# A two-model program on one core: TensorE's instructions in the order of the source, in place of the scheduler's order

## The chip, the cores and the metric

The program runs on one core of one Trainium2 chip. The metric is the device time of one execution in microseconds (us), the median of several runs. A core has five engines with instruction queues of their own: TensorE (PE: matrix products; its weight loads are listed apart as PEld), VectorE (DVE), ScalarE (ACT), GpSimd (POOL) and SyncE (SP, which here only starts transfers). Sixteen DMA engines bring the weights from memory.

## The reference

Two models run one after the other's parts on 256 tokens of width 1024. The first is one hybrid block (state-space scan, sparse attention, mixture of 32 experts), the second two layers that work on a sequence `x` and a context `ctx` (grouped-query attention, then latent attention, each with a convolutional feed-forward network). Cut to what matters here:

```
hn = rmsnorm(h) * (1 + scale1) + shift1               # ada = silu(c) @ w_ada gives shifts, scales, gates
y_ssm = mamba2(hn @ w_z, hn @ w_xbc, hn @ w_dt) @ w_ssm_out
y_nsa = nsa(hn @ w_q, keys, values, gates) @ w_nsa_out
h = h + gate1 * ((sigmoid(hn @ w_gs) * y_ssm + sigmoid(hn @ w_ga) * y_nsa) @ w_o)
hn2 = rmsnorm(h) * (1 + scale2) + shift2
for e in range(32):                                    # two experts of each token count
    out += combine[:, e] * ((silu(hn2 @ w_g[e]) * (hn2 @ w_u[e])) @ w_d[e])
h = h + gate2 * out
# second model, per layer: x, ctx += gate * mixer(norm(x), norm(ctx)); x, ctx += gate * ffn(...)
# layer 0: q, k = rms_norm per head, rope on x; softmax(q k^T) v over ctx and x keys; layer 1: MLA
out = final norms of both, joined
```

All inputs are fp32, and the products are held close to fp32.

## The kernel before

**Products.** A dense product is worked in groups of 512 KB to 1 MB of weights. `weight` starts a transfer from SP's queue into one of 14 buffers `raw` (256 KB each); ScalarE rounds it into `whi` (L212), VectorE puts the rest into `wlo` (L213), four buffers of each; `mm3` then issues three matmuls (L241, L242, L243: whi by the high part, wlo by the high part, whi by the low part). The three stand for one product below and are called a triple. `lin_fm` issues 8 triples for a group, 256 columns wide; `lin_tm` does the same with tokens on the partitions. `behind` holds the products of a group back in the source until the split of the next group has been issued, and evictions of a finished sum are put off in the same way (`late`, `flush`).

**Small matmuls in fours.** Experts get 32 rows of a 128-row tile each: `expert_block` issues for every slice of the contraction four fp32 matmuls of 32 columns, one for each expert of the unit, that write different quarters of one bank (L1346 for gate and up, L1368 for down). The modulation vectors (L417) do the same with four slices of 512 columns. These are called quads below. The trace counts an fp32 matmul as two instructions, so that a whole quad is x8 there and x4 in the order of the program.

**The order of the work.** The source is written as generators. `weave` advances one (the main one) and after each step lets the others (fills) run for the cost that the step announced, by shares written in the code (`CTX`, `COST`, `Gap`). So products that wait for nothing but their weights stand in the source between the steps of chains that wait for other engines. This is not the order that runs: the Tile framework's scheduler orders each engine's instructions anew when the program is built, by its own estimate of when an operand is ready and with the source's order as the priority. The order is fixed then; at run time every engine goes through its queue in order.

**The stages.** First `first_act` and `project_tm` (dense projections, up to 79 us), then `project_xbc`, the gates `ssg` and `sga` with the scan (`ssd`) and the sparse attention (`nsa`) woven in, the scan's norm (`ssd_norm`, L798 and L548), the output products, the router, the experts (to about 1077 us) with the context half of layer 0 woven in, the attention of layer 0 on `x` (heads: norm, rope, transposes L1632; scores L1744), its feed-forward part, layer 1 and the final norms. In the experts stage `experts_rest` is a conditional block (`tc.If`) that runs only if an expert was chosen more often than its places allow.

Of the kernel before, what the change touches and what calls it, by code (L numbers as in the profile page):

```python
# [107 lines left out]
class Kernel:  # L108
# [932 lines left out]
    def tanh_gates(self, act, c0, sg):  # L1041
# [2 lines left out]
            self.A.activation(sg[:, m, :], ps, AF.Tanh, scale=0.5)  # L1044
        yield from self.lin_fm(self.I["w_in"][0], c0, D, act, ev)

    def mark(self, name):
        self.marks.append(name)

    def first_block(self, rb):  # L1050
        V, A, T, I = self.V, self.A, self.T, self.I
        h = self.h
        act, pss = self.first_act(rb)
        self.mark("tm")
        self.drain(self.project_tm(act, pss))
        self.rope_tables()
        self.ssd_dt()
        self.mark("xbc")
        self.load_vecs([3, 4, 5, 6, 7])
        for i in range(2):  # L1060
            self.take_bias(self.fetch_bias(self.I["ada_b_2"][i]), self.ada2[i])
        prep = self.nsa_prepare()
        self.mix(self.project_xbc(act), (prep, 0.1))
        self.drain(prep)

        def nsa():
            yield from self.nsa_compress()
            self.nsa_cmp_probs()
            yield 2.0
            yield from self.nsa_attend()  # L1070
        ssg = self.sb("F", [P, 8, TOK], name="ssg")
        nsa_g, ssd_g, ada_g = nsa(), self.ssd(), self.ada_rest
        self.mark("ssg")
        self.mix(self.tanh_gates(act, 6992, ssg), (ssd_g, 0.7), (nsa_g, 0.35), (ada_g, 0.3))
        sga = self.sb("G", [P, 8, TOK], name="sga")
        self.mark("sga")
        self.mix(self.tanh_gates(act, 8016, sga), (ssd_g, 0.6), (nsa_g, 0.35), (ada_g, 0.3))
        self.drain(ssd_g)
        self.mark("z")
        sums = [self.sb(f"cbm{i}", [P, 2, TOK], name="sums") for i in range(2)]  # L1080
        self.mix(self.ssd_gate(act, sums), (nsa_g, 0.55), (ada_g, 0.3))
        self.drain(nsa_g)
        self.mark("norm")

        def ev_a(m, ps):
            V.scalar_tensor_tensor(sga[:, m, :], sga[:, m, :], 1.0, ps, OP.add, OP.mult)
        norm = self.ssd_norm(sums)
        self.mix(self.lin_fm(I["w_nsa_out"][0], 0, D, self.nsa, ev_a), (norm, NORM), (ada_g, 0.2))
        self.drain(norm)
        self.mark("out")  # L1090

        class Two:
            def __init__(self, ts):
                self.ts = ts

            def __getitem__(self, key):
                _, k, s = key
                return self.ts[k // 8][:, k % 8, s]

        mh, ml = self.pair("B", [P, 8, TOK])  # L1100

        def ev_s(m, ps):
            V.scalar_tensor_tensor(ssg[:, m, :], ssg[:, m, :], 1.0, ps, OP.add, OP.mult)
            V.tensor_tensor(sga[:, m, :], sga[:, m, :], ssg[:, m, :], OP.add)
            self.evict_split(mh[:, m, :], ml[:, m, :], sga[:, m, :])
        self.mix(self.lin_fm(I["w_ssm_out"][0], 0, D, (Two(self.y_hi), Two(self.y_lo)), ev_s), (ada_g, 0.3))
        self.drain(ada_g)
        ctx = self.layer0_ctx_in()
        next(ctx)
        g = self.sb("s", [P, 8])  # L1110
        V.tensor_scalar(g, self.ada1[:, 0, 16:24], 0.5, None, OP.mult)
        self.mix(self.residual(I["w_o"][0], (mh, ml), h, g), (ctx, CTXIN))
        self.drain(ctx)
        self.dbg("h1", h)
# [197 lines left out]
    def expert_weights(self, part, experts):  # L1312
# [20 lines left out]
        return tiles  # L1333

    def expert_block(self, xg, d, q, experts, sizes):

        V, A, T = self.V, self.A, self.T
        tiles = [slice(sum(sizes[:j]), sum(sizes[:j + 1])) for j in range(len(sizes))]
        acc = self.ps("acc", [P, 512])
        for i in range(4):  # L1340
            for n in "gu":
                ws = self.expert_weights(n + str(i), experts)
                c0 = 256 * (n == "u")
                for k in range(2):
                    for r, w in zip(tiles, ws):
                        T.matmul(acc[r, c0:c0 + 256], xg[:, 2 * i + k, P * q + r.start:P * q + r.stop], w[:, k, :],  # L1346
                                 start=(n == "g" and i == 0 and k == 0), stop=(i == 3 and k == 1), skip_group_check=True)
                yield COST[len(sizes)]
# [61 lines left out]
    def experts(self):  # L1410

        xs, first, n = {}, {}, 0
        for unit in sorted(UNITS.split()):
            first[unit] = n
            n += len(SIZES.get(unit, [32] * 4))
        for unit in UNITS.split():
            d, q = int(unit[0]), int(unit[1])
            if d not in xs:
                xs[d] = self.expert_gather(d, f"XB{len(xs) % 2}")
                yield 1.0  # L1420
            sizes = SIZES.get(unit, [32] * 4)
            ids = self.ids(self.order, range(first[unit], first[unit] + len(sizes)))
            yield from self.expert_block(xs[d], d, q, ids, sizes)
            if unit == REST:
                self.experts_rest()

    def experts_rest(self):

        self.settle()
        total = self.nc.values_load(self.over[0:1, 16:17], min_val=0, max_val=16)  # L1430
        with self.tc.If(total > 0):
            for d in (6, 7):
                xg = self.expert_gather(d, f"XB{d % 2}")
                for q in range(2):
                    n = 8 * (d - 6) + 4 * q
                    self.drain(self.expert_block(xg, d, q, self.ids(self.over, range(n, n + 4)), [32] * 4))
# [487 lines left out]
    def run(self):  # L1924
        with self.tc.tile_pool(name="sb", bufs=1) as self.pool:
            self.setup()
            self.h = self.sb("hx", [P, 8, TOK])
            self.ada1 = self.sb("ada1", [P, 1, 48])
            self.ada2 = [self.sb(f"ada2{i}", [P, 2, 48]) for i in range(2)]
            for tag in SHARED:  # L1930
                if tag == SHARED[tag]:
                    self.sb(tag, [P, 8, TOK])
            with self.phase(cw2=2, pb=5, pT=2), self.banks(lin=2, fl=1, S=2, aux=2, acc=1):
                first = [self.fetch_vecs(0)]
                x = self.fetch_tm(self.I["x"][0], "C", self.A)
                self.take_vecs([0], first)
                self.ada_stat()
                bias = self.fetch_bias(self.I["b_ada"][0])
                first = [self.fetch_vecs(1)]
                self.turn_fm(x, self.h)  # L1940
                self.load_constants(0)
                rb = self.sb("rb", [P, TOK])
                self.V.tensor_copy(rb, self.rms_bcast(self.h, 8, D))
                self.take_vecs([1], first)
                self.take_bias(bias, self.ada1)

                def rest():
                    yield from self.ada_first([1, 2])
                    yield from self.ada_second(0)
                self.ada_rest = rest()  # L1950
                self.first_block(rb)
            with self.phase(k4=4, m=3, fg=2, hT=2):
                with self.banks(lin=2, S=2, aux=2, acc=2):
                    self.load_constants(1)
                    self.mark("router")
                    ctx = self.layer0_ctx()
                    self.mix(self.router(self.h), (ctx, CTX[0]))
                    self.mark("experts")
                    self.mix(self.experts(), (ctx, lambda: CTX[1 + self.room // 2]))
                    self.mark("L0")  # L1960
                    self.mix(self.layer0_x_attend(), (ctx, lambda: CTX[3 + (self.att is not None)]))
                    self.mark("ctx rest")
                    self.drain(ctx)
                with self.banks(lin=4, fl=1, aux=2, acc=1):
                    self.mark("L0 rest")

                    def side():
                        yield from self.ada_second(1, Q2)
                        yield from self.layer1_ctx()
                    ctx = side()  # L1970
                    self.mix(self.layer0_x_rest(), (ctx, 0.5))
                    self.drain(ctx)
                    self.ada_last = self.ada_second(1, Q3)
                    self.mark("L1")
                    self.drain(self.layer1_x())
                    self.finish()


# [29 lines left out]
```

## Time and profile before

| what | value |
|---|---|
| median of three runs | 1915.17 us (1913.99, 1915.17, 1926.64) |
| the profiled execution, its own time | 1915.28 us |
| its span | 1913.5 us, so 1.8 us lie around it |
| PE, PEld, DVE, ACT busy | 95%, 74%, 67%, 48% |
| DMA | 381.53 MB, mean 199 GB/s |
| mean granted TensorE clock | 0.975 of full speed |

The busy time of an engine is the time in which at least one of its instructions runs, by a model of the ends for PE. The clock is a share of 2.4 GHz, the higher of two levels. Rows of a timeline give the start, the duration, the engine, the line and the operation, output before inputs; neighbours of one kind are merged, with their count behind x.

### The profile page before, as it was taken

The page shows a single profiled execution, that of the slowest core. Times are in us where ns is not written, and L with a number is a line of the kernel's source. Part 1 is how long each engine was busy: PE and PEld are TensorE (multiplying, and loading weights), DVE is VectorE, ACT ScalarE, POOL GpSimd, SP SyncE. Part 2 cuts the span into 40 slices and gives each one's busy share as a digit, 9 for nine tenths or more (in the row PEclk, how much of TensorE's full clock was granted, in tenths as well). Part 3 has the DMA queues.
Part 4 walks back from the last instruction along what each step waited for, and adds up shares of the span by engine and source line. Part 5 has one row for each costly group of instructions (what it writes and reads, how often), then busy time and mean ns, then how long its engine had stood idle before and what let it go on. Part 6 is the DMA issues. An engine that isn't in the chain of part 4 may idle for free.

```text
span 1913.5 us, 36458 instructions
## 1 busy us (share of the span) xinstructions
PE 1810.3 (95%) x12928; PEld 1411.7 (74%) x12928; DVE 1274.4 (67%) x3074; ACT 916.2 (48%) x1893; POOL 41.5 (2%) x48
## 2 busy tenths in 40 slices
PE   7999999999979989989989998998999989989998
PEld 3897767678855578756555675767999966479998
DVE  3997787765786367444433678837877877468776
ACT  3666457733544234212212356635655655347654
POOL 0000000100010000000000010000000000000000
PEclk9999999999999989999989998998999999999999
DMA  9757866579527949949787451274566553476662
GB/s 309 206 144 250 267 191 213 186 233 319 165 94 238 324 138 340 347 152 335 254 257 243 138 147 53 75 245 133 171 182 183 154 166 125 146 220 185 183 183 82
DMA packets 344961, 381.53 MB, mean 199 GB/s; under 512 B 27353, under 2 KB 298454, under 8 KB 344774
## 3 DMA queue, kind: packets, MB, share of 16 engines
q1 hardware_dynamic: 339456, 376.47, 63.2%
q10 hardware_dynamic: 5174, 1.97, 0.4%
q8 instruction: 104, 1.70, 0.4%
q14 instruction: 83, 0.68, 0.1%
q0 software_dynamic: 144, 0.71, 0.1%
HBM read 378.00 MB, written 1.05 MB: 198 GB/s over the span
## 4 chain that ended last, share of the span: by engine, by line
PE 47%; DVE 3%; DMA 2%; ACT 2%; issue 1%; POOL 1%; SPq 0%; POOLq 0%; DVEq 0%; ACTq 0%
PE lin L242 11%; PE lin L241 11%; PE lin L243 10%; PE acc L1346 3%; PE fl L417 2%; PE acc L1559 2%; PE acc L1368 2%; PE lin L1878 1%; PE aux L1551 1%; PE S L1744 1%; DMA raw<-in_ada_w_dram 1%; PE aux L1401 1%; DVE wlo L213 0%; POOL s L1612 0%; PE aux L1824 0%
## 5 line engine op out<-in xcount | busy, mean ns | idle before, releaser
L212 ACT CAST whi<-raw 128x512 fp32r<-128x512 f32 (+2 forms) x752 | 452.3, 610 | 446.3 <-PE lin L243 290.3
L213 DVE TENSOR_TENSOR wlo<-raw,whi 128x512 fp32r<-128x512 f32 (+2 forms) x752 | 501.8, 677 | 182.7 <-ACT whi L212 171.5
L241 PE MATMUL lin<-XA,whi 128*128 128x256 f32 x832 | 238.5, 287 | 2.2 <-ACT XA L494 2.2
L242 PE MATMUL lin<-XA,wlo 128*128 128x256 f32 x832 | 237.3, 285 | 0.0
L243 PE MATMUL lin<-XA,whi 128*128 128x256 f32 x832 | 237.0, 285 | 0.0
L241 PE MATMUL lin<-A,whi 128*128 128x256 f32 x576 | 168.3, 292 | 3.4 <-DVE k L627 3.4
L241 PEld LDWEIGHTS lin<-XA,whi 128*128 128x128 f32 x832 | 161.0, 194 | 9.9 <-issue 5.0
L242 PEld LDWEIGHTS lin<-XA,wlo 128*128 128x128 f32 x832 | 161.0, 194 | 4.0 <-issue 2.5
L242 PE MATMUL lin<-A,wlo 128*128 128x256 f32 x576 | 163.6, 284 | 0.0
L243 PEld LDWEIGHTS lin<-XA,whi 128*128 128x128 f32 x832 | 160.9, 193 | 0.6 <-issue 0.4
L241 PEld LDWEIGHTS lin<-A,whi 128*128 128x128 f32 x576 | 110.0, 191 | 31.6 <-ACT whi L212 11.7
L241 PE MATMUL lin<-CA,whi 128*128 128x256 f32 x416 | 125.8, 303 | 6.1 <-ACT whi L212 5.6
L242 PE MATMUL lin<-CA,wlo 128*128 128x256 f32 x416 | 126.7, 305 | 3.0 <-DVE wlo L213 2.8
L243 PE MATMUL lin<-A,whi 128*128 128x256 f32 x448 | 127.9, 285 | 0.0
L243 PE MATMUL lin<-CA,whi 128*128 128x256 f32 x416 | 123.6, 297 | 0.0
L1678 ACT ACTIVATE cv<-lin,vecs 128x256 f32<-128x256 f32 x132 | 73.8, 559 | 82.6 <-PE lin L243 67.3
L242 PEld LDWEIGHTS lin<-A,wlo 128*128 128x128 f32 x576 | 110.1, 191 | 1.3 <-issue 1.0
L1679 DVE SCALAR_TENSOR_TENSOR cv<-lin,vecs,cv 128x255 f32<-128x255 f32 x132 | 63.3, 479 | 69.1 <-ACT cv L1678 68.0
L1346 PE MATMUL acc<-wx,xg 128*32 128x256 f32 x896 | 104.9, 389 | 0.0
L417 PE MATMUL fl<-raw,stat 128*32 128x512 f32 x512 | 100.1, 603 | 2.5 <-DMA raw<-in_ada_w_dram 2.3
L241 PEld LDWEIGHTS lin<-CA,whi 128*128 128x128 f32 x416 | 81.5, 196 | 27.0 <-issue 15.7
L242 PEld LDWEIGHTS lin<-CA,wlo 128*128 128x128 f32 x416 | 81.5, 196 | 26.3 <-issue 19.6
(539 smaller groups left out, 3874.9 us busy)
## 6 DMA issues: line engine op xcount, KB each, us to landing
raw<-in_ffn_w_up_dram SPq DMA_DIRECT2D x264, 256.0 KB
raw<-in_ada_w_dram SPq DMA_DIRECT2D x192, 256.0 KB
raw<-in_ffn_w_down_dram SPq DMA_DIRECT2D x132, 256.0 KB
raw<-in_w_in_dram SPq DMA_DIRECT2D x112, 256.0 KB
wx<-in_w_exp_gate_dram SPq DMA_DIRECT2D x112, 256.0 KB
wx<-in_w_exp_up_dram SPq DMA_DIRECT2D x112, 256.0 KB
wx<-in_w_exp_down_dram SPq DMA_DIRECT2D x112, 256.0 KB
raw<-in_w_ada_dram SPq DMA_DIRECT2D x96, 256.0 KB
```

Source lines behind the costliest of these rows:

```text
L212: self.A.copy(hi, raw)
L213: self.V.tensor_tensor(lo, raw, hi.bitcast(F32), OP.subtract)
L241: mm(out, whi, ahi, start=first, stop=False, skip_group_check=True)
L242: mm(out, wlo, ahi, start=False, stop=False, skip_group_check=True)
L243: mm(out, whi, alo, start=False, stop=last, skip_group_check=True)
L417: self.T.matmul(acc[32 * j:32 * j + 32, :], self.stat[:, k, :], self.weight(W[k * P:k * P + P, c:c + 512]), start=(k == 0), stop=(k == 7), ...
L1346: T.matmul(acc[r, c0:c0 + 256], xg[:, 2 * i + k, P * q + r.start:P * q + r.stop], w[:, k, :], start=(n == "g" and i == 0 and k == 0), stop ...
L1368: T.matmul(out[r, c0:c0 + 256], hT[:, k, r], w[:, k, :], start=(c0 == 0 and k == 0), stop=(k == 1), skip_group_check=True)
L1401: self.T.matmul(pc[:, i, :], o[:, part, ms], comb, start=(i + part == 0), stop=(part == 1), skip_group_check=True)
L1559: T.matmul(po[64 * a:64 * a + 64, :], V_fn(2 * i + a, k), pTs[i][a][:, k, :], start=(k == 0), stop=(k == nkt - 1), skip_group_check=True)
L1678: A.activation(acc, ps, AF.Identity, bias=self.v(f"fb{i}", m), scale=self.v(f"fw{i}1", m))
L1679: V.scalar_tensor_tensor(acc[:, 1:], ps[:, 0:TOK - 1], self.v(f"fw{i}0", m), acc[:, 1:], OP.mult, OP.add)
```

## The change

The change wraps most of the program in `manual_schedule` for TensorE: within it PE's instructions keep the order in which the source issues them. The other engines' instructions are still ordered by the scheduler. The region begins after `first_act` (the first dense product and its sums), is left around the conditional block and entered again behind it, and ends ahead of the last norm (`finish`).

```
+    def pin(self, on=True):
+
+        if on:
+            self.pinned = self.tc.manual_schedule(engines={mybir.EngineType.PE})
+            self.pinned.__enter__()
+        else:
+            self.pinned.__exit__(None, None, None)
...
         act, pss = self.first_act(rb)
+        self.pin()
         self.mark("tm")
...
             if unit == REST:
+                self.pin(False)
                 self.experts_rest()
+                self.pin()
...
                     self.drain(self.layer1_x())
+                    self.pin(False)
                     self.finish()
```

The lines behind it move: L1346 becomes L1355, L1368 becomes L1377, L1632 becomes L1643, L1744 becomes L1755. The rows below show the order of one engine, here always PE; a name with a number is one buffer.

In an expert unit, beginning of the down product, before (CB: the context product woven in; XB and wx: experts):

```order
L1355 MATMUL aux<-ident,k_13287 128x128 x2
L1386 MATMUL aux<-ident,hots 128x128 x2
L1368 MATMUL acc<-wx,hT 32x256 x8
L241 MATMUL lin<-CB_11842,whi 128x256
L242 MATMUL lin<-CB_11842,wlo 128x256
L243 MATMUL lin<-CB_11843,whi 128x256
L241 MATMUL lin<-CB_11842,whi 128x256
L1368 MATMUL acc<-wx,hT 32x256
L242 MATMUL lin<-CB_11842,wlo 128x256
L243 MATMUL lin<-CB_11843,whi 128x256
L241 MATMUL lin<-CB_11842,whi 128x256
L1368 MATMUL acc<-wx,hT 32x256
```

The same place after:

```order
L1355 MATMUL acc<-wx,xg 32x256 x8
L1364 MATMUL aux<-ident,k_13292 128x128 x2
L1395 MATMUL aux<-ident,hots 128x128 x2
L1377 MATMUL acc<-wx,hT 32x256 x8
L241 MATMUL lin<-CB_11847,whi 128x256
```

Before, single matmuls of a quad stand between the matmuls of the triples; after, two whole quads stand together and 8 triples follow them. The two transposes of the unit's middle (L1355 before, L1364 after) have no product between themselves and the quads on either side after.

In the heads of layer 0 on x, at the end of the last of three chunks of queries, before (S<-whi,XA: the chunk's product; CA: the context's product):

```order
L241 MATMUL S<-whi,XA_13644 128x512
L242 MATMUL S<-whi,XA_13645 128x512
L243 MATMUL S<-wlo,XA_13644 128x512
L242 MATMUL lin<-CA_8412,wlo 128x256
L1744 MATMUL S<-kT_6565,qTx 128x512
L243 MATMUL lin<-CA_8413,whi 128x256
L1744 MATMUL S<-kT_6565,qTx 128x512
L241 MATMUL lin<-CA_8412,whi 128x256
```

And after:

```order
L241 MATMUL S<-whi,XA_13649 128x512
L242 MATMUL S<-whi,XA_13650 128x512
L243 MATMUL S<-wlo,XA_13649 128x512
L1643 MATMUL aux<-ident,pr 128x128 x8
L548 MATMUL aux<-k_14297,ones 128x256
L1755 MATMUL S<-kT_6567,qTx 128x512 x6
L241 MATMUL lin<-CA_8414,whi 128x256
```

Before, 15 more triples of the context stand ahead of the chunk's transposes (L1632); after, the transposes follow the chunk's last product at once, and the triples stand behind the first scores.

At the end of the sparse attention, which is drained there with no product of the main generator left, before (L970 scores, L1002 transposes of probabilities, L1009 and L1015 sums over values, D: the next dense product):

```order
L1009 MATMUL acc<-pcT,vblk 128x256
L1002 MATMUL aux<-ident,prob 128x128 x8
L970 MATMUL S<-kT,qT 128x256 x2
L417 MATMUL fl<-raw,stat 32x512 x3
L241 MATMUL lin<-D_3031,whi 128x256
L1015 MATMUL acc<-pT,vt 64x256 x2
```

And after:

```order
L970 MATMUL S<-kT,qT 128x256 x2
L1002 MATMUL aux<-ident,prob 128x128 x4
L970 MATMUL S<-kT,qT 128x512 x2
L1002 MATMUL aux<-ident,prob 128x128 x8
L1009 MATMUL acc<-pcT,vblk 128x256
L1015 MATMUL acc<-pT,vt 64x256 x2
```

Before, the next head's scores stand ahead of the last head's sums, and 8 triples of the next dense product and 5 modulation matmuls lie among the last three heads; after, each head is finished before the next begins, and nothing lies between.

## Rows read from the trace of the kernel before

**Rows 1.** The page's first lines: the span, and PE's busy time.

```profile
span 1913.5 us, 36458 instructions
PE 1810.3 (95%) x12928; PEld 1411.7 (74%) x12928; DVE 1274.4 (67%) x3074; ACT 916.2 (48%) x1893; POOL 41.5 (2%) x48
```

**Rows 2.** PE's waits: total us, times, longest us.

```profile
PE S L1744 <- ACT prob L1532: 9.5, 4, 6.5
...
PE aux L1632 <- DVE pr L1509: 4.9, 3, 2.3
...
PE aux L1355 <- DVE k L1352: 3.4, 6, 1.3
```

**Rows 3.** Groups by line: busy us, mean ns of one, idle before.

```profile
L1346 PE MATMUL acc<-wx,xg 128*32 128x256 f32 x896 | 104.9, 389 | 0.0
L417 PE MATMUL fl<-raw,stat 128*32 128x512 f32 x512 | 100.1, 603 | 2.5 <-DMA raw<-in_ada_w_dram 2.3 <-DMA raw<-in_w_ada_dram 0.2
L1368 PE MATMUL acc<-wx,hT 128*32 128x256 f32 x448 | 55.3, 389 | 2.1 <-DVE hT L1357 2.1
```

**Rows 4.** Timeline of PE in the experts stage.

```profile
1002.39 0.62 PE L1368 MATMUL acc<-wx,hT 128*32 128x256 f32 x2
1002.94 0.38 PE L241 MATMUL lin<-CA,whi 128*128 128x256 f32 x1
...
1006.51 1.05 PE L1368 MATMUL acc<-wx,hT 128*32 128x256 f32 x10
1007.50 0.38 PE L242 MATMUL lin<-CA,wlo 128*128 128x256 f32 x1
```

**Rows 5.** Timeline of PE where the sparse attention is drained.

```profile
359.08 1.13 PE L970 MATMUL S<-kT,qT 64*128 64x512 f32 x4
360.14 1.07 PE L417 MATMUL fl<-raw,stat 128*32 128x512 f32 x8
361.13 1.09 PE L1002 MATMUL aux<-ident,prob 128*128 128x128 f32 x8
...
367.33 1.04 PE L417 MATMUL fl<-raw,stat 128*32 128x512 f32 x2
368.41 0.67 PE L1009 MATMUL acc<-pcT,vblk 128*128 128x256 f32 x2
```

**Rows 6.** Stretches: length, PE, PEld, DVE, ACT, POOL busy, clock, DMA share, GB/s.

```profile
710.00:810.00 100.00, 98.67 (x824) 77.45 (x824) 61.13 (x144) 33.57 (x65) 0.00 (x0) 1.00 1.08 343
...
900.00:1050.00 150.00, 138.44 (x889) 80.64 (x888) 58.70 (x131) 35.66 (x72) 0.00 (x0) 0.95 0.81 254
...
577.00:1077.00 500.00, 471.37 (x3361) 312.99 (x3360) 242.27 (x584) 139.69 (x289) 0.70 (x1) 0.96 0.82 258
```

**Rows 7.** Stretches again, just behind two gaps of PE.

```profile
684.00:696.00 12.00, 8.20 (x40) 5.48 (x41) 8.19 (x22) 3.00 (x7) 0.70 (x1) 0.59 0.17 50
1304.00:1312.00 8.00, 3.28 (x10) 1.62 (x10) 4.14 (x11) 0.89 (x2) 0.69 (x1) 0.50 0.23 71
```

**Rows 8.** Timeline of PE where the second projection ends.

```profile
79.43 0.36 PE L241 MATMUL lin<-A,whi 128*128 128x256 f32 x1
...
84.06 1.03 PE L840 MATMUL aux<-ident,qkv 128*128 128x128 f32 x8
```

**Rows 9.** Timeline of PE in the heads of x: two chunks' last products, and their transposes.

```profile
1105.88 0.39 PE L243 MATMUL S<-wlo,XA 128*128 128x512 f32 x1
...
1111.39 0.66 PE L1632 MATMUL aux<-ident,kd 128*128 128x128 f32 x4 [0.67 <-DVE kd L1509]
...
1121.87 0.39 PE L243 MATMUL S<-wlo,XA 128*128 128x512 f32 x1
...
1132.31 0.63 PE L1632 MATMUL aux<-ident,pr 128*128 128x128 f32 x4 [2.27 <-DVE pr L1509]
```

**Rows 10.** Timeline at the scan's norm: the sums, and the broadcast of the roots.

```profile
386.09 1.95 PE L798 MATMUL aux<-ones,sums 128*128 128x1 f32 x16
...
391.63 1.05 PE L548 MATMUL aux<-k,ones 128*128 128x512 f32 x1
```

## The prediction

> **What bounds the kernel now.** I read the page's first lines, then PE's waits, the groups by line, the stretches, and last the timelines at the places that the order shows to move. PE is busy for 1810 of 1913.5 us [rows 1], so there are 103 us of gaps in all, and the longest waits on PE's list take 3 to 10 us in total [rows 2]. Over most of the program PE's queue is therefore the bound, and the change touches it alone: it can win only by making PE's own work shorter, and lose only by putting waits into it that other products hide today. The reader is to see both in the rows. "Busy" hides the first: two groups of small matmuls, L1346 and L417, count as over 100 us each [rows 3], and part of that is waste. One stage has a second bound: from 710 to 810 us the DMA runs at 343 GB/s, which is as fast as it gets here, while from 900 to 1050 us it gives 254 [rows 6].
>
> **What a broken quad costs.** In the experts stage one matmul of 32 columns alone (x2) takes 0.55 us from its start to the next product's, a run of five (x10) 0.99 us [rows 4]. Five are one round of four and one more, so a run costs 0.55 for its first round and 0.44 for each further one, whether a round holds one matmul or four: the members of a quad run beside each other, and a member on its own costs as much as the quad. The same for L417: a single member (x2) takes 1.08 us, a whole quad (x8) 0.99 [rows 5].
>
> **The change part by part: gains.** Counted in the order, outside the conditional block (this execution does not run it: the trace has 896 instructions of L1346 in quads, 448 matmuls [rows 3], and the program 704 with the block's 256):
> - L1346, before: 74 runs of one to four matmuls (66 of them singles), 40 of five to eight, one of ten, 7 of sixteen: 74 x 0.55 + 40 x 0.99 + 1.43 + 7 x 1.87 = 95 us. After: one short run, 16 of eight, 20 of sixteen: 54 us. That is 41 us less.
> - L1368, before: 45 short runs, 23 of five to eight, 2 of eleven, one of sixteen: 52 us. After: 4 short, 18 of eight, 5 of sixteen: 29 us. That is 23 us less, and 64 with the first.
> - How much of the 64 reaches the clock? Where the DMA is at its peak, nothing. From 900 to 1050 us the bytes would take 150 x 254 / 343 = 111 us at peak, so up to 39 us can go there; I let all of it go, since PE is busy for 138 of those 150 us and many of the singles stand there. Of the other 25 us I take 17, since the units' middles now stand bare: two transposes wait for a Silu and a product, which cost 0.6 us each time before where they were bare (3.4 us in 6) [rows 2]. So the term is **-56 us**, with ends of -30 (only part of the 39) and -64.
> - L417: 76 runs become 54, nearly all whole quads. 22 runs at about 1.0 us are -22; they stand beside chains that may end last anyway, so I take **-20**, ends 0 and -22.
>
> In the two feed-forward stages the order of PE is the same triples one after another, and I cost the change there at nothing with PE busy throughout: the splits on ScalarE and VectorE hide under it, and if they fell behind, the wait would be for whi or wlo.
>
> **The change part by part: losses.** A chain that leaves PE, goes over VectorE, ScalarE or GpSimd and comes back is covered now by whatever the scheduler found ready. In the source's order the instruction behind it waits at the head of PE's queue, and all products behind it wait with it.
> - Start of the third projection: the transposes L840 stand ahead of all its products after, while 13 triples run in their shadow before, from 79.43 to 84.06 us [rows 8]: **+4.5**, ends 4 and 5.
> - Scan and sparse attention: the source puts a group of 8 triples between most steps, so I take +6 (0 to 16) for the steps that need more. In the drained end, from 359 us to the scan's norm at 386 us, 8 triples at about 0.36 us and the broken quads (some 4 us) fill the gaps of the last heads [rows 5, 10]; they come behind after, and each head waits for the one ahead: +10 (6 to 14). Together **+16**, ends 6 and 30.
> - Scan's norm: L798 at 386.09, L548 at 391.63, with GpSimd's root between them [rows 10]. The sums themselves take 2 us, the 3.5 us behind are filled with triples now: +3. The norms ahead of the output product and of the router are the same chain with the mean of squares: +6 for both, an estimate by this row. **+9**, ends 4 and 11.
> - Heads of x in layer 0: from a chunk's last product to its transposes there are 5.5 us for the keys (1105.88 to 1111.39) and 10.4 for the first queries (1121.87 to 1132.31), of which PE idled 0.67 and 2.27 [rows 9]. Part of the second is queueing on VectorE behind splits, which a stalled PE takes away. After, the transposes follow at once. Three chunks at 5 to 8 us, less the gaps that are there already, would be 15; the triples that now stand later shorten the attention's own waits for L1744 (9.5 us) [rows 2], so **+12**, ends 5 and 22. The context's heads, which are better covered, **+3** (0 to 8).
> - Layer 0's rest and layer 1: norms of the latent vectors, with a group of products between the steps in most places: **+6**, ends 2 and 16.
>
> Sum of the losses: 4.5 + 16 + 9 + 12 + 3 + 6 = 50.5, ends 21 and 92.
>
> **Sum.** -56 - 20 + 50.5 = -25.5 against the profiled execution's own 1915.28, which is the median of the runs but for 0.1: **1890 us**. The ends together: -64 - 22 + 21 = -65 (1850) and -30 + 92 = +62 (1977).
>
> **The rivals.**
> - *The bare chains decide (slower).* Each wait that the scheduler hides today is exposed, at the upper prices: 92 us of losses against 50 to 76 of gains is +16 to +42, 1931 to 1957. It has a place: the heads of x and the drained attention, 10 to 35 us each or together. For it: PE idles only 103 us now, so very little of all these chains shows, which says that the cover is worth much. Against it: the source puts products between most steps, one group apart. It decides from some 75 us of losses on.
> - *The clock follows the gaps (slower too).* Behind PE's gaps the granted clock is low: 0.59 in the 12 us from 684 us and 0.50 in the 8 us from 1304 us [rows 7], the lower level of 1.2 GHz for most of them. A stretch of 8 us at half clock loses 4 us of work. If each of the three bare chains of the heads, two of the norms and two of layer 1 brings that, it is 7 x 4 = 28 us on top: 1918. [...] The Trainium skill, in "TensorE: Matmul & The Clock Gate", section "Why this matters for your kernels", asks for no idle gaps of PE between bursts, as the clock falls to its lower level behind them; by that rule this rival's 28 us would come with the forecast's stalls, and the two rows agree with it as far as they go.
> - *The DMA keeps the gain (no change).* If the freed PE time in the experts only waits for weights, the gain there is 30 us, and the sum -30 - 20 + 50 = 0: 1915. For it: the DMA's share is 0.82 over that whole stage and 1.08 in parts. Against it: 254 GB/s from 900 us on, where most broken quads stand [rows 6].
> - *It does not do what it says.* The order shows that the quads are whole; I leave this at nothing.
>
> **How the numbers follow.** The forecast, a gain of over 1%, has 0.47. No change, by the DMA or by chains that eat the gain, has 0.24. The bare chains at their upper prices have 0.17 and the clock 0.12; the clock's sum alone is 1918, but it comes with dearer chains if it comes, so I count it to the slower side with them. Faster by over 1% is thus 0.47, within 1% 0.24, slower by over 1% 0.29; 1% is about what a measurement of this kernel can tell from no change. The forecast's own range is 1850 to 1900. The whole one is 1848 to 1962: it takes in the forecast, no change and most of the bare chains, and leaves out the highest prices of all terms together, and the little below the forecast's best sum.
>
> **What the changed profile would show.** The quads: no x2 rows of L1355 and L1377 but x16 and x32, their busy sums near 70 and 35 us where L1346 and L1368 have 105 and 55 [rows 3], and the stage that ended at 1077 us some 40 us shorter, net of what comes ahead of it. The losses: new rows among PE's waits, L840 or L846 on VectorE once with 4 us, L1643 with 12 to 20 us in 3 or more times where L1632 has 4.9, L548 with over 10, L1002 or L1009 with several us. The clock: below 1.00 in the stretches behind those. The feed-forward stages equal to a us. I am wrong if PE's sum of gaps grows by more than 75 us, or if the experts stage does not shrink although its quads are whole.

## The result, and the profile after

The changed kernel takes 2011.34 us (median of four runs, 2008.79 to 2020.52), the kernel before 1917.81 (four runs): a ratio of 1.0489, with a 95% interval of 1.0438 to 1.0541. It is slower by about 94 us, where 1890 us was forecast, and lies above the range's upper end of 1962.

The page's first lines of the changed kernel answer to [rows 1]:

```profile
span 2006.9 us, 36462 instructions
PE 1750.8 (87%) x12928; PEld 1425.2 (71%) x12928; DVE 1294.0 (64%) x3074; ACT 917.5 (46%) x1885; POOL 41.2 (2%) x48
```

PE is busy 60 us less than before, for the same 12928 matmuls, and yet the span is 93 us longer: the gaps of PE went from 103 to 256 us. The mean granted clock fell from 0.975 to 0.939. Busy time at a lower clock holds less work. Summed over stretches of 4 us, busy time times what the clock lacks of full speed is 38 us before and 87 after. So the 93 us are an account with three entries: work at full clock 1772 to 1664 (-109), gaps 103 to 256 (+153), clock 38 to 87 (+49). The third entry is a count and not yet a price: of the four runs one shows a mean clock of 0.892 where the others show 0.937 to 0.939, which is 93 us more of lower clock over its span, and it took only some 10 us longer (2020.52).

Where the 93 us lie is read from stretches that hold nearly the same work in both kernels (the counts of matmuls differ by at most 62). Columns as in [rows 6]: length; busy time of PE, PEld, DVE, ACT, POOL; clock; DMA share; GB/s. The six stretches begin at the third projection, the output product behind the first block's two halves, the first expert product, the final norm's sums ahead of the heads of x, the end of the attention of layer 0, and the last feed-forward part. Before:

```profile
84.00:478.00 394.00, 388.21 (x3046) 307.90 (x3046) 292.33 (x753) 219.30 (x481) 11.52 (x14) 1.00 0.71 224
478.00:585.00 107.00, 94.08 (x568) 76.72 (x570) 82.59 (x235) 53.54 (x122) 9.98 (x8) 0.94 0.37 116
585.00:1077.00 492.00, 463.37 (x3323) 306.03 (x3321) 237.78 (x571) 136.82 (x280) 0.70 (x1) 0.97 0.83 262
1077.00:1250.00 173.00, 159.62 (x938) 118.34 (x937) 137.36 (x324) 102.19 (x207) 10.26 (x8) 0.95 0.33 96
1250.00:1678.00 428.00, 411.49 (x2845) 335.01 (x2841) 298.19 (x690) 230.26 (x480) 6.05 (x9) 0.98 0.56 171
1678.00:1913.00 235.00, 222.21 (x1820) 218.62 (x1820) 175.47 (x341) 136.22 (x257) 1.40 (x2) 0.98 0.57 168
```

And after:

```profile
83.00:545.00 462.00, 405.73 (x3108) 322.53 (x3107) 304.73 (x767) 218.61 (x483) 12.14 (x15) 0.93 0.62 195
545.00:668.00 123.00, 97.18 (x536) 80.42 (x540) 77.67 (x214) 49.50 (x108) 9.69 (x7) 0.83 0.29 84
668.00:1092.00 424.00, 374.93 (x3328) 285.12 (x3322) 243.78 (x579) 143.60 (x288) 0.69 (x1) 0.96 0.96 303
1092.00:1305.00 213.00, 163.87 (x916) 126.39 (x914) 138.94 (x320) 99.60 (x203) 9.88 (x8) 0.86 0.27 80
1305.00:1765.00 460.00, 416.66 (x2863) 345.05 (x2859) 302.24 (x691) 232.88 (x482) 5.75 (x9) 0.96 0.52 159
1765.00:2006.00 241.00, 224.31 (x1819) 219.99 (x1818) 176.08 (x341) 136.66 (x257) 1.40 (x2) 0.98 0.55 163
```

The lengths differ by +68, +16, -68, +40, +32 and +6 us. Only the experts got shorter: PE's busy time there fell by 88 us and the DMA rose from 262 to 303 GB/s. In the other five PE's busy time rose by 2 to 18 us, and the gaps grew: 6 to 56 us in the first stretch, 13 to 49 in the fourth.

PE's waits in the changed kernel (total us, times, longest) answer to [rows 2]:

```profile
PE S L1755 <- ACT prob L1543: 23.2, 8, 5.1
PE aux L1643 <- DVE pr L1520: 19.5, 2, 9.7
PE aux L548 <- DVE k L545: 16.5, 9, 2.9
PE aux L733 <- DVE k L727: 15.6, 10, 2.8
PE aux L1792 <- DVE junk L1788: 12.1, 5, 2.9
...
PE aux L950 <- DVE scmp L946: 5.8, 1, 5.8
...
PE aux L1643 <- DVE kd L1520: 5.3, 1, 5.3
```

All of these are waits for VectorE or ScalarE, on chains that leave PE and come back. The heads' transposes (L1643, before L1632) wait 9.7 us twice and 5.3 once. The segment sums of the scan (L733) are new on the list. The latent norms (L1792) were L1781 before, with 2.0 us in all:

```profile
PE aux L1781 <- DVE junk L1777: 2.0, 5, 0.7
```

The quads, for [rows 3], by line: busy us, mean ns of one.

```profile
L417 PE MATMUL fl<-raw,stat 128*32 128x512 f32 x512 | 81.5, 630 | 2.3 <-DMA raw<-in_ada_w_dram 2.3
L1355 PE MATMUL acc<-wx,xg 128*32 128x256 f32 x896 | 66.2, 384 | 1.8
L1377 PE MATMUL acc<-wx,hT 128*32 128x256 f32 x448 | 33.2, 401 | 3.5 <-DVE hT L1366 3.2
```

They need 81.5, 66.2 and 33.2 us where they needed 100, 105 and 55, for the same counts.

### The profile page after: what moved, and what is told of

It reads as the page before. It is cut to its first block, busy times and chain, and to the rows that moved or that the text cites. A ratio compares the mean times of both kernels' runs of the same rounds, so it can differ in the third digit from the quotient of the medians.

```text
span 2006.9 us, 36462 instructions
## 1 busy us (share of the span) xinstructions
PE 1750.8 (87%) x12928; PEld 1425.2 (71%) x12928; DVE 1294.0 (64%) x3074; ACT 917.5 (46%) x1885; POOL 41.2 (2%) x48
## 4 chain that ended last, share of the span: by engine, by line
PE 40%; DVE 6%; DMA 4%; ACT 3%; issue 1%; POOL 1%; SPq 0%; POOLq 0%; DVEq 0%; ACTq 0%
PE lin L241 10%; PE lin L242 10%; PE lin L243 9%; PE acc L1570 2%; PE fl L417 1%; DMA wx<-in_w_exp_gate_dram 1%; PE lin L1889 1%; PE S L1755 1%; DVE wlo L213 1%; DVE s L1537 1%; PE acc L1355 1%; PE aux L1562 1%; ACT prob L1543 1%; DMA raw<-in_ffn_w_up_dram 1%; PE S L241 1%
## 5 line engine op out<-in xcount | busy, mean ns | idle before, releaser
L241 PEld LDWEIGHTS lin<-XA,whi 128*128 128x128 f32 x832 | 163.2, 196 | 7.7 <-issue 4.2
L243 PEld LDWEIGHTS lin<-XA,whi 128*128 128x128 f32 x832 | 162.9, 196 | 0.3
L241 PEld LDWEIGHTS lin<-A,whi 128*128 128x128 f32 x576 | 112.8, 196 | 34.9 <-issue 19.4
L242 PE MATMUL lin<-CA,wlo 128*128 128x256 f32 x416 | 120.7, 290 | 1.3 <-DVE wlo L213 1.3
L241 PE MATMUL lin<-XB,whi 128*128 128x256 f32 x352 | 101.2, 288 | 7.0 <-ACT XB L235 7.0
L243 PE MATMUL lin<-XB,whi 128*128 128x256 f32 x352 | 101.4, 288 | 1.0 <-DVE XB L236 0.7
L242 PE MATMUL lin<-XB,wlo 128*128 128x256 f32 x352 | 100.3, 285 | 0.0
L243 PEld LDWEIGHTS lin<-A,whi 128*128 128x128 f32 x448 | 88.2, 197 | 0.0
```

Of the source, the lines that this page charges most:

```text
L241: mm(out, whi, ahi, start=first, stop=False, skip_group_check=True)
L242: mm(out, wlo, ahi, start=False, stop=False, skip_group_check=True)
L243: mm(out, whi, alo, start=False, stop=last, skip_group_check=True)
```

## The experiments

The theory after the result: the change acts stage by stage. In the experts stage whole quads shorten PE's work; everywhere else the kept order puts bare chains at the head of PE's queue, and the gaps lower the clock on top. Rivals: the loss is one of the program as a whole, the short experts stage is only a wait that moved, the clock is only seen and costs nothing of its own. The kernels with an interval ran four times each, the pair with the zero weights twice, the others once. Each ran on the same chip as repeats of the kernel before, whose medians there are 1911 to 1915 us, not 1917.81. A gain on the changed kernel is therefore given with two ends: by the times themselves, and by the distances to the kernel before.

**The order kept in one part only.** First block alone:

```
                 self.first_block(rb)
+                self.pin(False)
...
-                self.pin(False)
                 self.experts_rest()
-                self.pin()
```

(The last `pin(False)` is taken out too.)

> TensorE's order is kept only from the second projection to the end of the first block's attention and scan part (before the router). Theory (stage by stage: bare chains cost, whole quads win, each in its own stage): the first products of the output projection start 67 us later than before, as in the changed kernel, all else as before, so about 1982 us (1970 to 1992). Rival (the loss comes from the program as a whole, through weights that arrive later or another buffer allocation): well under half of the 67, below 1950, or more than the 94 us of the whole change.

Measured: 1977.21 us, 63 above the kernel before. Experts alone (`pin` after `first_act` and the last `pin(False)` taken out):

```
                     self.mark("experts")
+                    self.pin()
                     self.mix(self.experts(), (ctx, lambda: CTX[1 + self.room // 2]))
+                    self.pin(False)
```

> The order is kept only in the experts stage. Theory: whole quads save what that stage saved in the changed kernel, 69 us, and nothing else moves: about 1848 us (1835 to 1865), faster than both kernels. Rival (that stage was short only because the router part ahead of it was late and weights had already arrived, a wait that was moved): 1895 to 1920.

Measured: 1848.45 us, a ratio of 0.9666 (0.9646 to 0.9687). The experts' stretch, from the first expert product to about the final norm's sums:

```profile
585.00:1010.00 425.00, 375.09 (x3332) 286.05 (x3331) 245.56 (x580) 143.83 (x287) 0.70 (x1) 0.97 0.96 305
```

It is the changed kernel's stretch but for a microsecond, with the stages ahead of it as they were before: nothing was moved into it. From layer 0's attention on alone (`self.pin()` behind `self.mark("L0")`, the last `pin(False)` kept):

> The order is kept only from the attention of layer 0 to the last norm but one. Theory: the losses of the heads (30), the attention (11), layer 0's rest and layer 1 (31) and the end (7) come back as they are: about 1995 us (1980 to 2005). Rival (these stages are late because of what stands ahead of them): below 1950.

Measured: 1987.95 us, +74. The three parts add up to 63 - 66 + 74 = +71; with the 16 us of the stretch between them, which none of the three holds in full, +87 of the +94. So the stages add up but for 7 us, with two of the three parts run once, and a rival that needs the whole program has no room beyond that.

**Scan and sparse attention freed.** The changed kernel, with `pin(False)` at `mark("ssg")` and `pin()` ahead of `mark("norm")`:

> The changed kernel, but TensorE's order is the scheduler's from the gates' first group to the end of the sparse attention (scan, attention and the products woven with them). Theory: most of the first block's loss is there: some 45 us less than the changed kernel, 1955 to 1975. Rival (the loss is in the third projection ahead of it and in the output products behind): 1990 to 2010.

Measured: 1963.45 us, 41 to 48 less than the changed kernel; in its trace the first expert product starts 48 us sooner (619.25 against 667.72). So most of the first block's 63 to 68 us lies in the scan, the attention and what is woven with them.

**The clock.** The changed kernel, with fillers ahead of three kinds of waiting instructions, for instance at the scan's sums:

```
                     pseg = self.ps("aux", [P, 4, P])
+                    for i in range(10):
+                        T.transpose(pseg[:, i % 4, :], self.ident, self.ident)
```

> The changed kernel, with transposes of the identity put ahead of three kinds of waiting instructions on TensorE (10 ahead of each of the scan's segment sums, 48 ahead of the compressed probabilities' transposes, 40 to 70 ahead of each chunk's transposes in the heads of x); they write a tile that is overwritten. They fill gaps that are there anyway. Theory that the clock is a cost of its own beside the gaps (22 us in the scan and attention stage, 22 in heads and attention): some 20 us less than the changed kernel, 1980 to 1995, and a granted clock of 0.95 or more. Rival (the gaps are all, a lower clock is only seen in them): 2008 to 2020, as the fillers take a little time of their own.

Measured: 1998.16 us, 10 to 13 less, between the two expectations and nearer to the theory's: PE does more and the program ends earlier. The first stretch of the changed kernel's table, in this kernel:

```profile
83.00:545.00 462.00, 423.52 (x3374) 344.02 (x3374) 311.52 (x782) 224.39 (x492) 12.17 (x15) 0.97 0.62 197
```

Its clock is 0.97, not 0.93, and by the sum over 4-us stretches the clock's share of the whole span fell from 87 to 72 us. So a part of that entry is a cost of its own, about as large as the time won; the rest (router, layer 1) had no fillers.

**Cover written into the source.** First the context's share in the heads:

```
-CTX = 1.2, 2.1, 1.3, 0.15, 0.6
+CTX = 1.2, 2.1, 1.3, 0.6, 0.6
```

> The changed kernel with one number of the weave changed, the context's share in the heads of x (0.15 becomes 0.6), so that four times as many of the context's products stand in the source among the heads. Theory (a bare chain costs what no product covers, so cover written into the source repairs it): the 33 us that the heads wait for their transposes shrink by 10 to 20, the attention behind gets less cover and loses up to 8, the clock gives a few us: 1985 to 2002 us. Rival (products are only moved, what the heads gain the attention loses): 2004 to 2018.

Measured: 1996.15 us, 8 to 15 less than the changed kernel; the heads' two waits of 9.7 us are 13.5 together. Then a step of the weave ahead of the transposes as well:

```
+            yield 1.0
             tp = self.ps("aux", [P, 4, P])
             for j in range(4):
                 src = kd[:, j].rearrange("p a d -> p (a d)") if isk else pr[t][:, c0 + j * P:c0 + j * P + P]
```

> The changed kernel with cover written into the source at the heads: a step of the weave between a chunk's last work on VectorE and its transposes on TensorE, and the context's share in the heads at 0.6 as before. Theory (bare chains are the loss, and products in front of them repair it): waits of the heads' transposes fall from 25 us to under 10, 1975 to 1992 us. Rival (the chunk's chain is bound by VectorE and GpSimd and not by what stands in TensorE's queue): as with the share alone, 1993 to 2003.

Measured: 1976.49 us, 31 to 35 less than the changed kernel. PE's waits at those transposes there:

```profile
PE aux L1644 <- DVE pr L1520: 9.8, 1, 9.8
...
PE aux L1644 <- DVE kd L1639: 0.5, 1, 0.5
```

Counting the context's heads too they fell from 37 us to 10, and one, behind the last chunk of x, is as long as before: the context's next 8 triples stand behind it and not in front. That chain is no shorter; at the others products stand in front. The same in the scan:

```
-                    yield 0.5
+                    yield None
                     pseg = self.ps("aux", [P, 4, P])
```

> The changed kernel with cover written into the source of the scan: each of the 16 segment sums lets the main generator issue a group of products first. Theory: the 19 us of waits at the segment sums fall below 6, and with the clock the time falls by 10 to 30: 1980 to 2000 us. Rival (the gates have too few products: the scan ends later and its rest is drained bare): 2005 to 2030.

Measured: 2000.73 us, 7 to 11 less, just outside the theory's range. The wait at L733 fell from 15.6 to 9.7 us: in this trace the last 6 of the 16 sums have no product of the gates in front (4 in the changed kernel), so part of the scan is still drained bare.

**What the quads save.** The order inside a quad, on the kernel with the experts alone:

```
-                for k in range(2):
-                    for r, w in zip(tiles, ws):
+                for r, w in zip(tiles, ws):
+                    for k in range(2):
```

> The kernel with the order kept in the experts stage alone, but the two slices of one expert stand behind each other, so that neighbours write the same 32 columns: of 8 matmuls of two quads (2 rounds) it makes 5 rounds. Same matmuls, same results, no product between them. Theory (a quad saves because its members run beside each other): some 84 groups of 8 cost 3 more rounds of 0.44 us each, 111 us of TensorE time, of which the weights' transfers hide some 20: 1930 to 1960 us. Rival (the saving is of the changes between products and quads, or of the order of transfers): 1845 to 1875.

Measured: 1851.96 us, no change beside 1848. The expectation was the theory's own, and it was wrong: a group of 8 takes as long in either order, and the time lies where the rival put it, which laid the saving to the changes between products and quads. PE's timeline in this kernel:

```profile
726.27 1.09 PE L1354 MATMUL acc<-wx,xg 128*32 128x256 f32 x16
727.29 0.39 PE L241 MATMUL lin<-CA,whi 128*128 128x256 f32 x1
```

From start to start it is 1.02 us; with the members side by side it is 1.01 (721.49 to 722.50). What matters is then that the members stand together, not in which order. Whether it is this that saves was tried with a pair of kernels that hold the same 63 added matmuls of zero weights, once inside a group and once behind it (there the condition is `k == 1 and r.start == 96`):

```
                         T.matmul(acc[r, c0:c0 + 256], ...)
+                        if len(ws) == 4 and k == 0 and r.start == 0 and (n, i) != ("g", 0):
+                            T.matmul(acc[:, c0:c0 + 128], self.zero, w[:, k, 0:128], start=False, stop=False, skip_group_check=True)
```

> The kernel with the order kept in the experts stage, with 63 added matmuls of a full-width zero weight (they add zeros to the open sum) that stand behind the first member of a group of 8: each group is broken into 1 and 7, nothing else moves. Theory (a member broken off costs a round of its own, 0.55 us): 63 x 0.5 = 32 us of TensorE time more than the same matmuls behind the group, of which the weights' transfers hide up to half: 16 to 32 us above its partner. Rival (what the kept order saved was not the quads): within 8 us of its partner.

> Partner of the run before: the same 63 added matmuls, but behind the last member of each group of 8, so that the quads stay whole. The price of the added matmuls alone, 63 x 0.3 to 0.6 us: 1855 to 1885 us by both theories.

Measured: 1876.37 us broken (1875.25, 1877.48), 1857.15 with the quads whole (1853.13, 1861.18): 19 us between them. PE's timeline in the broken one:

```profile
737.79 0.62 PE L1354 MATMUL acc<-wx,xg 128*32 128x256 f32 x2
738.34 0.49 PE L1357 MATMUL acc<-wx,zero 128*128 128x128 f32 x2
738.76 1.07 PE L1354 MATMUL acc<-wx,xg 128*32 128x256 f32 x16
739.76 0.49 PE L1357 MATMUL acc<-wx,zero 128*128 128x128 f32 x2
740.17 1.06 PE L1354 MATMUL acc<-wx,xg 128*32 128x256 f32 x14
```

The member broken off costs its own 0.55 us from start to start, as in [rows 4]; where two groups follow each other the seven left over join the next one's first member, so only some groups pay, and the 32 us expected of TensorE came to 20. Whether a lone member's price is its own round or the change from narrow to full-width matmuls on either side of it, these runs do not separate.

**Products not held back.** The kernel with the experts alone, with each group's products issued right behind its split in that stage:

```
+        if self.now and products:
+            self.ahead = None
+            products()
```

> The kernel with the order kept in the experts stage alone, but there a group's products are issued right behind their own weights' split, not one group later. Theory (kept order needs the products one group behind, else TensorE waits for each split at the head of its queue): about a group's split of 4 us exposed in part for each of some 50 groups, so waits for whi and wlo grow from nearly nothing to 40 to 100 us and the time to 1885 to 1940. Rival (splits run ahead anyway since transfers and buffers allow it): 1845 to 1862.

Measured: 1850.00 us, no change, where the theory had at least 1885. PE's waits for the splits appear, but add up to 18 us and not to 40 or more:

```profile
PE lin L245 <- ACT whi L213: 9.0, 7, 2.8
PE lin L246 <- DVE wlo L214: 8.6, 13, 2.1
```

That they do not lengthen the stage fits its DMA share of 0.95 from 585 to 1010 us, but was not tried by itself. In that stage "one group later" is worth nothing that can be measured; it was not tried elsewhere.

**A version that beats both.** Experts alone, with one more step in each unit:

```
         V.tensor_tensor(hh, hh, acc[:, 256:512], OP.mult)
+        yield Gap(1.5)
```

> The kernel with the order kept in the experts stage alone, with one step more in each expert unit: a gap of 1.5 us announced to the weave between the unit's Silu product and its two transposes, so that a group of the context's products stands there. Theory (the unit's middles are bare): the 9 us of waits at the transposes and some of the 8 at what follows go, 1834 to 1843 us. Rival (the stage is held by the weights' transfers now, 299 GB/s over it): 1845 to 1853.

Measured: 1832.62 us, a ratio of 0.9579 (0.9557 to 0.9601): 13 to 16 us less than without that step, more than the 9 us of waits at the transposes. At the transposes of the units' middles 0.9 us of waits are left. One step more, ahead of each combination (`yield 0.5` becomes `yield Gap(1.0)`):

> The kernel with the order kept in the experts stage and the middles covered, with a gap of 1.0 us announced ahead of each combination as well, so that products stand between the eviction of an expert's sum and the matmuls that combine it. Theory: most of the 12 us of waits there go, 1820 to 1829 us. Rival (transfers bound the stage now, or the context's products run out earlier): 1830 to 1838.

Measured: 1836.97 us, a ratio of 0.96 (0.9575 to 0.9626): no gain, as the rival said. The runs do not separate its two reasons.

## Why the prediction was wrong

- **The gain was right in kind, and its size near.** The experts' term, -56 us with ends of -30 and -64, measured -68 in the changed kernel and -66 when the order is kept there alone. That broken quads cost time is shown by the pair of zero-weight kernels, 19 us for 63 breaks. That they make most of the gain is read from the lines: of the 88 us that PE's busy time fell in the experts' stretch, 61 are L1346 and L1368, and 18 the triples that they stood among. The DMA did not keep the gain: it went to 303 GB/s. The picture that the expectation of the reordered members had, that neighbours must write different columns, was wrong, and did not enter the sum. The term for L417, -20, shows as 18.6 us less busy time of that line; in the stretches where it lies the chains took more than it gave, and what it is worth alone was not tried.
- **The step that failed is the sum of the losses**, 50.5 us with ends of 21 and 92. The five stretches that grew hold +162. The rival of the bare chains, with a chance of 0.17, named the right side, but its 92 us were too few as well.
- *Scan and sparse attention, +16 (6 to 30).* Freeing that part gives back 41 to 48. Most of it is not the drained end, which had +10 of the 16. In the changed kernel the third projection's first product, the first step of the drained end and the scan's norm start here ([rows 8, 5, 10] have them at 79.43, 359.08 and 386.09 before):

```profile
86.02 0.36 PE L241 MATMUL lin<-A,whi 128*128 128x256 f32 x1
...
407.48 1.13 PE L970 MATMUL S<-kT,qT 64*128 64x512 f32 x4
...
433.71 1.95 PE L798 MATMUL aux<-ones,sums 128*128 128x1 f32 x16
```

The woven part and the drained end as stretches, before:

```profile
79.43:359.08 279.65, 275.10 (x2210) 222.05 (x2210) 221.00 (x566) 167.88 (x360) 7.65 (x10) 1.00 0.68 211
359.08:386.09 27.01, 25.77 (x180) 15.33 (x179) 20.69 (x92) 18.30 (x59) 2.20 (x3) 1.00 0.44 136
```

And after:

```profile
86.02:407.48 321.46, 281.47 (x2190) 227.13 (x2189) 221.18 (x540) 159.17 (x348) 7.59 (x10) 0.93 0.59 181
407.48:433.71 26.23, 20.96 (x146) 12.29 (x145) 18.86 (x89) 17.28 (x57) 2.19 (x3) 1.00 0.28 88
```

The drained end's gaps grew from 1 to 5 us, so of its +10 about 4 came. The woven part grew by 42 us, 35 of them gaps (5 to 40), where the step had +6 (0 to 16). The step said that the source puts a group of 8 triples between most steps. It does put one there, but a share of the weave lets the scan take two or three steps at a time, so a chain that leaves and returns within these steps has no cover: ten waits at L733 alone are 15.6 us, L950 another 5.8.
- *Start of the third projection, +4.5.* The place is there, and about as large: L840 starts at 82.71 after, without its cover, and the first product of the projection at 86.02 instead of 79.43. (The cover was 10 triples by the trace, not 13.)
- *Heads of x, +12, and the context's, +3.* The stretch from the heads to the end of attention grew by 40. I read 5.5 and 10.4 us off [rows 9] and then took off the gaps that were there, a queue on VectorE that would vanish, and a gain in the attention behind. The waits measured 5.3, 9.7 and 9.7: the rows had the price, and the discounts were wrong. Nor did the attention gain: of L1744's 9.5 us only 1.3 lie in the attention on x (the rest is the context's attention), and there L1755 waits 15.7 us after.
- *Layer 0's rest and layer 1, +6.* It is +32; L1792 alone waits 12.1 us. The last feed-forward part, put at nothing, is +6. The norms, router and output product, +9, are +16 in the second stretch, besides the norm in the first. One wait there had no term at all: transposes of the context's input (L388) stand at the head of PE's queue for 5.8 us until a transfer lands.
- **The clock was a rival, and should have been a term.** I gave it 28 us and a chance of 0.12 as an addition. It is 49 us in the account, and fillers in a part of the gaps bought 10 to 13 back; that all 49 are time lost is not shown. The rows that it rested on were there [rows 7], and it came again, as here behind a wait of 9.7 us in the heads:

```profile
1152.00:1156.00 4.00, 0.52 (x3) 0.55 (x4) 3.97 (x12) 0.00 (x0) 0.00 (x0) 0.50 0.00 0
1156.00:1160.00 4.00, 4.00 (x12) 3.22 (x11) 1.45 (x3) 1.21 (x2) 0.00 (x0) 0.50 0.00 0
```

So by these rows the price of a bare chain is its wait plus what PE loses at half clock behind it. The rule of the Trainium skill, in "TensorE: Matmul & The Clock Gate", section "Why this matters for your kernels", that PE should have no idle gaps between bursts, held here: 0.86 in the fourth stretch after, with 49 us of gaps, 0.95 before, with 13.
- **The test that I set was the right one**: wrong "if PE's sum of gaps grows by more than 75 us". It grew by 153. The forecast counted each gain over the whole order, run by run, but each loss only at places that I had picked, with a row for the place and a discount by judgement. A count of every instruction that has no product between itself and the chain that it waits for would have been possible from the same order.

## What to carry to other kernels

Where a scheduler orders an engine's queue, keep the order by hand only in stages whose time something else may set (here perhaps the transfers, at a DMA share of 0.96), and look there for matmuls that run together and were pulled apart: here that stage gave 66 us, and 79 with one step more; the rest of the same change took 160. Price every chain that leaves the engine and comes back by its full length, from its last product to its return, plus the clock behind the gap; discount it only by products that stand in the order between the two. Before keeping an order, write the cover into the source: one step ahead of the heads' transposes and a larger share there gave 31 to 35 us, one step in the experts' middles 13 to 16.

## What the runs showed of the hardware

A full group of 8 matmuls of 32 columns takes 1.02 us from start to start when neighbours write the same columns, and 1.01 when they write different ones; a single one set between full-width matmuls takes 0.55. That the order inside a group does not matter was not expected.
